# Low parts of the odd layer's q and k weights made by an accumulating DMA instead of a VectorE subtraction

## The chip, the cores and the metric

One core of a Trainium2 chip runs the kernel. The metric is device time in microseconds (us) of one execution; for the kernel before the runs gave 977.92 and 978.41 us, median 978.16. The profile is of one execution, and its times count from that execution's first instruction.

## The reference

A trunk of two layers over 256 tokens of width 2048, all in float32. The even layer joins sparse attention and stick-breaking attention; the odd layer is differential attention with eight heads:

```python
def _odd_layer(x, w_in, ...):
    q, k, v, gate = _split(x @ w_in, ODD_SIZES)          # 4 x 2048 columns
    o = _diff_attn(q, k, v, ...) * jax.nn.silu(gate)     # per head two q and two k of 128, one v of 256
    return _layer_norm(DEEPNORM_ALPHA * x + o @ w_out, ln_g, ln_b)
```

What the change touches is the product of x with the 4096 columns of q and k in the odd layer.

## The kernel before, in words

Products are made on TensorE from numbers in two parts. `split` (L125) turns a float32 tile w into a high part h (a cast to float32r on ScalarE, L126) and a low part l = w - h (a subtraction on VectorE, L127). A product then takes three matmuls: h with the high part of x, h with the low part of x, l with the high part of x.

The weights come once from HBM, in tiles of 128 x 2048 float32 (1 MB). `load_split` (L146) takes a raw tile (three buffers, `wr`), loads it by a DMA from SyncE's queue (L150), and for each half of 1024 columns takes a buffer `wh` and a buffer `wl` (four of each, so four halves or two tiles in all) and splits into them.

In the odd layer's q and k stage, `diff_proj` (L745) calls `ws_pair` (L185) for q and for k of a head, each of two `ws_block`s (L176). A block is one weight tile with 16 chunks of 128 x 128; each chunk is the stationary operand of three matmuls over the 256 tokens (L181 to L183), 48 matmuls to a block. So a head has four blocks, eight halves, and there are eight heads: 32 tiles, 64 halves. L182 is the last reader of a `wh` buffer, L183 of a `wl` buffer. After each block, stages of the attention of the heads before (`diff_attn`, L758) are let in: scores, softmax (`softmax_rows`, L333), transposes, the product with v.

The q and k tiles are then turned by `rope` on VectorE (L297 to L300) and split again. Before this stage lies the odd layer's v projection (`odv` in the names), behind it the gate projection (`odg`) and the output projection (`oo`); these go through `xs_group` with `load_split`, as do the even layer's projections.

Each engine works its own queue in order, and so does SyncE's DMA queue; a framework places instructions on the queues and inserts the waits. The trace shows the loads, casts and subtractions of a tile well ahead of the matmuls that use it, as far as buffers are free. GpSimd (POOL) does only four memsets' worth of setup at the start.

Of the kernel before, what the change touches and what calls it, by code (L numbers as in the profile page):

```python
# [11 lines left out]
F32R = mybir.dt.float32r  # L12
# [4 lines left out]
SEQ = 256  # L17
# [14 lines left out]

# columns of ev_w_in: q kc vc ks vs kw vw gates gate_a qb kb vb gate_b
_SIZES = (1024, 256, 256, 256, 256, 256, 256, 24, 1024, 1024, 1024, 1024, 1024)
_NAMES = ("qa", "kc", "vc", "ks", "vs", "kw", "vw", "ga", "gate_a", "qb", "kb", "vb", "gate_b")
_OFF = dict(zip(_NAMES, np.cumsum((0,) + _SIZES[:-1]).tolist()))
# stationary-weight column blocks of the even layer, in the order they are used
EV_WS = (["kc", "vc", "ks", "kw"], "qa", "qb", "kb", "gate_a", "gate_b")
EV_XS_W = 390

# packed constants: name -> (offset, width)
_CW = (("cosq", 256), ("sinq", 256), ("cosk", 256), ("sink", 256), ("mpos", 256), ("mneg", 256),
# [41 lines left out]
def hybrid_trunk(ctx: ExitStack, tc: tile.TileContext, a):  # L84
# [9 lines left out]
    NU = 28  # L94
    # the one table set with all of Exp, Ln, Abs, Square, Copy and Identity
    nc.scalar.preload_act_table_set("natural_log_exp_and_others")
# [19 lines left out]

    # ---- zeros through the tensor engine while the first loads are under way, so that its clock is up
    zero = cpool.tile([P, 512], mybir.dt.bfloat16, name="zero")
# [4 lines left out]

    # ---- splitting float32 into two parts of 12 bits each, exactly
    def split(h, l, src):  # L125
# [3 lines left out]
    def mm3(o, lhs, rhs, start, stop):  # L129
        """o += lhs.T @ rhs, both in parts"""  # L130
        (ah, al), (bh, bl) = lhs, rhs
        nc.tensor.matmul(o, ah, bh, start=start, stop=False, skip_group_check=True)
        nc.tensor.matmul(o, ah, bl, start=False, stop=False, skip_group_check=True)
        nc.tensor.matmul(o, al, bh, start=False, stop=stop, skip_group_check=True)

    # ---- weights: one DMA per tile, then the two parts
    def raw_tile(n):
# [5 lines left out]
    def unit_part(name, n):  # L143
        return unit(name, [1024], F32R)[:, :n]

    def load_split(src, n, alloc=part, pieces=None, m=1):  # L146
        """pieces(j): called before each part of a half, which is then loaded and split by itself"""
        raw = raw_tile(n)
# [14 lines left out]

    # work in stages, one stage of each after every block of a projection
    staged = []
# [9 lines left out]

    def ws_block(src, ps, xh, xl):  # L176
        """ps[cols, tokens] = W[:, 128 cols].T @ x.T"""
        parts = load_split(src.rearrange("p k c -> p (k c)"), 2048)
        for k in range(NK):
            h, l = (t.rearrange("p (k c) -> p k c", c=P)[:, k % 8, :] for t in parts[k // 8])  # L180
            nc.tensor.matmul(ps, h, xh(k), start=(k == 0), stop=False)  # L181
            nc.tensor.matmul(ps, h, xl(k), start=False, stop=False)  # L182
            nc.tensor.matmul(ps, l, xh(k), start=False, stop=(k == NK - 1))  # L183

    def ws_pair(src, i, name, xh, xl):  # L185
        ps = acc(name)
        for c in range(2):
            ws_block(src[i + c], ps[:, c * SEQ:(c + 1) * SEQ], xh, xl)
            tick()
        return ps.rearrange("p (c t) -> p c t", c=2)  # L190
# [4 lines left out]
    def xs_mm(o, t, parts, half, k0, w, xh, xl, start, stop, c0=0):  # L195
        """o[tokens of t, cols] += x[:, two k] @ W[two k, cols]"""
        h, l = (p.rearrange("p (k c) -> p k c", c=w) for p in parts[half])
# [8 lines left out]
    def xs_group(src, w, name, xh, xl, ahead=None):  # L206
        """ps[t][tokens, cols] = x @ W[:, w cols]"""
        ps = [acc(f"{name}{t}") for t in range(NT)]
# [11 lines left out]
    def xs_apart(src, name, xh, xl, in_units, orders, ready, n_last=1, m=1):  # L220
        """like xs_group, one token tile after the other, the weights kept; ready(t, c0, ps) after each"""
        parts = [None] * 4
# [12 lines left out]

    # ---- constants
    cst = cpool.tile([P, NCST], F32, name="cst")
# [5 lines left out]

    # ---- x transposed, in parts
    def new_lhs(name):
# [30 lines left out]
    def load_constants():  # L276
        nc.sync.dma_start(cst, a["cst"])
        nc.sync.dma_start(sml, a["sml"])
        # lambda = exp(lq1.lk1) - exp(lq2.lk2) + lambda_init, negated, on every partition
        lqk = wk("lqk", [4, HD])  # L280
# [9 lines left out]

    # ---- helpers
    def rope(ps, cos, sin, out):
        """ps, out: [128 d, 2, 256 tokens]"""
        t1 = wk("rope1", [2, SEQ])
# [7 lines left out]
    def log_sigmoid_parts(g, w, tag):  # L302
        """e = ln(1 + exp(-|g|))"""
        e = wk(tag, [512])[:, :w]
# [17 lines left out]
    def rsqrt(out, v, n, name):  # L322
        """out = v ** -0.5, one Newton step after exp(-ln(v) / 2)"""
        y = small.tile([P, n], F32, name=name + "y")
# [8 lines left out]
    def softmax_rows(ps, n, mask, name):  # L333
        """ps: [128 q, 2, n] negated scaled scores -> unnormalised p and 1/sum for both."""
        sm = wk(name, [2, 256])
# [10 lines left out]
    def transposed(p, t, ps):  # L346
        """p: [128 q, (t+1)*128 keys] of query tile t into ps[keys, 3*128]: k0 t0 | k0 t1 | k1 t1"""
        for k in range(t + 1):
            o = (t + k) * P
            nc.tensor.transpose(ps[:, o:o + P], p[:, k * P:(k + 1) * P], ident)  # L350

    def add_pv(o, v, pT, start, stop):
        """o[d, 256 q] += v.T @ p.T over both key tiles"""
        nc.tensor.matmul(o, v(0), pT[:, 0:256], start=start, stop=False, skip_group_check=True)
        nc.tensor.matmul(o[:, P:], v(1), pT[:, 256:384], start=False, stop=stop, skip_group_check=True)

    # =========================== even layer ===========================
    ws, xs = a["ev_ws"], a["ev_xs"]
    # token-major columns: gates | vs | vw | vb
    vsw = [unit(f"vsw{i}", [NT, 512], F32R) for i in range(2)]  # L360
# [23 lines left out]

    kvT = unit("kvT", [2, 2, SEQ])  # compressed-branch k, v: [d, (k v), head, token]
    for i in range(2):
        ps = ws_pair(ws, 2 * i, f"kc{i}", xh, xl)
        nc.scalar.copy(kvT[:, i], ps)
    kr = [unit(f"kr{i}", [2, 2, SEQ], F32R) for i in range(2)]  # roped keys: [d, head, (select window), token]
    for i in range(2):  # L390
# [4 lines left out]

    # compression MLPs
    kcmpT = cpool.tile([P, 2, NCMP], F32, name="kcmpT")
    # compressed values: their three products of parts in one pass, the parts at rows 0, 32 and 64
    vcmp = cpool.tile([STACK, 2, HD], F32R, name="vcmp")
# [62 lines left out]

    # native sparse attention, two heads at a time
    oT = new_lhs("oT")
    hold = {}

    def held(i):
        """for the attention of heads 2i and 2i+1 of all 16"""
        if i // 2 not in hold:
# [13 lines left out]
    def nsa_attn(i, qc, qs):  # L483
        while 0 not in made:
            yield
        kv = i // 2
        # compressed branch
        sc = ps_s("sc")
# [18 lines left out]

        # selected and window branches
        def scores(h):
# [30 lines left out]
        nc.scalar.copy(pT[64:64 + NCMP], tc_[:NCMP, :])  # L540
        pk0 = [unit(f"pk0{j}", [2, 2, SEQ], F32R) for j in range(2)]  # [key, (select window), head, query]
        pk1 = [wk(f"pk1{j}", [2, 2, P], P, F32R) for j in range(2)]
# [72 lines left out]
    def gate_pair(i):  # L615
        """o = attention * silu(gate), in parts, for heads 2i and 2i+1 of all 16"""
        ps = ws_pair(ws, 32 + 2 * i, f"gate{i}", xh, xl)
# [20 lines left out]
    def cols(halves, c):  # L638
        """columns c * 512 ... of a row of 2048 kept in two units"""
        return halves[c // 2][:, c % 2 * 512:(c % 2 + 1) * 512]  # L640

    # ---- output projection, residual and layer norm
    def load_gb(g_src, b_src):
# [8 lines left out]
    def out_layer(wout, lhs, resid, name, finish, g=None, n_last=1):  # L652
        """resid[t] = alpha * resid[t] + lhs @ wout (times g), then finish(t, its mean and 1 / deviation)"""
        oh, ol = lhs_of(lhs)
# [46 lines left out]
    def normalise(t, scale, bias):  # L701
        """resid[t] becomes the normalised row, its scaled and shifted transpose goes to yT"""
        for c in range(4):
# [17 lines left out]

    # =========================== odd layer ===========================
    yh, yl = lhs_of(yT)
# [21 lines left out]
    def diff_proj(h):  # L745
        ps = ws_pair(ws, 4 * h, f"q{h}", yh, yl)
        q = wk("qr", [2, SEQ])
        rope(ps, C("cosq"), C("sinq"), q)
        ps = ws_pair(ws, 4 * h + 2, f"k{h}", yh, yl)
        k = wk("qc", [2, SEQ])  # L750
# [86 lines left out]
    def store(t, scale, bias):  # L837
        """resid[t] is r * g: r * g * scale + (g * bias + b)"""
        last = t == NT - 1
# [27 lines left out]
def _layout(x, ev_w_in, ev_pe_k, ev_pe_v, ev_w1_k, ev_w2_k, ev_w1_v, ev_w2_v, ev_w_out, ev_ln_g, ev_ln_b,  # L867
# [3 lines left out]
    def grouped(w, width):  # L871
        """[2048, n * width] -> [n, 128, 16, width]"""
        n = w.shape[1] // width
# [53 lines left out]
```

## Time and profile before

| | |
|---|---|
| median of the runs | 978.16 us (977.92 and 978.41) |
| span of the profiled execution, first to last instruction | 976.2 us |
| TensorE (PE) busy | 966.6 us, 99% |
| VectorE (DVE) busy | 668.7 us, 69% |
| ScalarE (ACT) busy | 505.6 us, 52% |
| GpSimd (POOL) busy | 1.2 us |
| moved by the DMA engines | 180.8 MB, 185 GB/s on the mean |
| q and k stage of the odd layer | about 582 to 783 us |

The profile has no total of its own beside the span; the runs' median lies 2.0 us above the span. PE stands for matmuls and PEld for the weight loads that overlap them. A DMA share of 1 means that all 16 DMA engines are busy all the time. In names such as `wl<-wr,wh` the tile written stands in front, the tiles read behind, and L127 is line 127 of the kernel before. Granted clock is given in parts of TensorE's full speed.

### The profile page before, as it was taken

The numbers are of one execution on the slowest core, as the hardware profiler recorded it, in microseconds if no ns is written. First come the engines' busy times: TensorE is split into PE (matmuls) and PEld (weight loads), VectorE is DVE, ScalarE is ACT, GpSimd is POOL, SyncE is SP. The second block draws the span as 40 slices with busy tenths as digits, with TensorE's granted clock in tenths as the row PEclk, the third lists the DMA queues.
The fourth block names the chain that finished last, engine by engine and source line by source line (L and its number), as shares of the span: only waits on it lengthen the run. The fifth ranks groups of instructions, "written<-read, shape, count | busy, mean of one in ns | idle before, by whom it ended". The sixth has DMA issues, their size and how long they took to land.

```text
span 976.2 us, 15916 instructions
## 1 busy us (share of the span) xinstructions
PE 966.6 (99%) x6497; PEld 891.6 (91%) x6497; DVE 668.7 (69%) x1107; ACT 505.6 (52%) x812; POOL 1.2 (0%) x8
## 2 busy tenths in 40 slices
PE   8999999999999999999999999999999999999998
PEld 6999999999999999988888889999999988888886
DVE  6544577695766856666598556777778776667676
ACT  5544444475657856535473443455545556664340
POOL 0000000000000000000000000000000000000000
PEclk9999999999999999999999999999999999999999
DMA  8765546643334345756547555544544445557542
GB/s 306 256 207 195 186 169 249 257 138 121 136 123 141 130 174 177 277 193 229 180 150 266 207 176 178 189 156 170 173 167 154 160 168 177 191 193 258 194 151 87
DMA packets 30457, 180.80 MB, mean 185 GB/s; under 512 B 3504, under 2 KB 5296, under 8 KB 11952
## 3 DMA queue, kind: packets, MB, share of 16 engines
q1 hardware_dynamic: 30384, 179.79, 52.3%
q8 instruction: 51, 0.84, 0.3%
q14 instruction: 22, 0.18, 0.1%
HBM read 177.68 MB, written 2.10 MB: 184 GB/s over the span
## 4 chain that ended last, share of the span: by engine, by line
PE 96%; DMA 1%; DVE 1%; ACT 1%; SPq 0%; issue 0%; DVEq 0%; ACTq 0%
PE k L182 3%; PE k L183 3%; PE k L181 3%; PE gate L183 3%; PE q L182 3%; PE gate L182 3%; PE gate L181 3%; PE q L181 3%; PE q L183 3%; PE oo L204 3%; PE oo L202 3%; PE oo L203 3%; PE odv L203 3%; PE odg L202 3%; PE odv L202 3%; PE odg L203 3%
## 5 line engine op out<-in xcount | busy, mean ns | idle before, releaser
L127 DVE TENSOR_TENSOR wl<-wr,wh 128x1024 fp32r<-128x1024 f32 (+3 forms) x330 | 383.2, 1166 | 225.1 <-ACT wh L126 217.9
L126 ACT CAST wh<-wr 128x1024 fp32r<-128x1024 f32 (+3 forms) x330 | 329.7, 1003 | 349.6 <-PE eo L204 40.9
L181 PE MATMUL q<-yTh,wh 128*128 128x256 f32 x256 | 72.9, 285 | 0.0
L181 PE MATMUL gate<-xTh,wh 128*128 128x256 f32 x256 | 72.8, 284 | 0.0
L183 PE MATMUL gate<-xTh,wl 128*128 128x256 f32 x256 | 72.5, 283 | 0.0
L181 PE MATMUL k<-yTh,wh 128*128 128x256 f32 x256 | 72.4, 283 | 0.0
L182 PE MATMUL k<-yTl,wh 128*128 128x256 f32 x256 | 72.4, 283 | 0.0
L183 PE MATMUL k<-yTh,wl 128*128 128x256 f32 x256 | 72.4, 283 | 0.0
L182 PE MATMUL gate<-xTl,wh 128*128 128x256 f32 x256 | 72.4, 283 | 0.0
L183 PE MATMUL q<-yTh,wl 128*128 128x256 f32 x256 | 72.4, 283 | 0.0
L182 PE MATMUL q<-yTl,wh 128*128 128x256 f32 x256 | 72.4, 283 | 0.0
L204 PE MATMUL oo<-wh,oT1l 128*128 128x512 f32 (+1 forms) x144 | 52.7, 366 | 0.0
L203 PE MATMUL oo<-wl,oT1h 128*128 128x512 f32 (+1 forms) x144 | 52.7, 366 | 0.0
L202 PE MATMUL oo<-wh,oT1h 128*128 128x512 f32 (+1 forms) x144 | 52.7, 366 | 0.0
L202 PE MATMUL odg<-wh,yTh 128*128 128x512 f32 x128 | 50.3, 393 | 0.0
L202 PE MATMUL odv<-wh,yTh 128*128 128x512 f32 x128 | 50.1, 392 | 0.0
L202 PE MATMUL eo<-wh,oTh 128*128 128x512 f32 x128 | 50.0, 391 | 0.0
L203 PE MATMUL odv<-wl,yTh 128*128 128x512 f32 x128 | 50.0, 390 | 0.0
L204 PE MATMUL odv<-wh,yTl 128*128 128x512 f32 x128 | 49.9, 390 | 0.0
L203 PE MATMUL eo<-wl,oTh 128*128 128x512 f32 x128 | 49.9, 390 | 0.0
L204 PE MATMUL odg<-wh,yTl 128*128 128x512 f32 x128 | 49.9, 390 | 0.0
L203 PE MATMUL odg<-wl,yTh 128*128 128x512 f32 x128 | 49.8, 389 | 0.0
(287 smaller groups left out, 2494.0 us busy)
## 6 DMA issues: line engine op xcount, KB each, us to landing
wr<-in_ev_ws_dram SPq DMA_DIRECT2D x48, 1024.0 KB, 4.8
wr<-in_od_xs_dram SPq DMA_DIRECT2D x32, 1024.0 KB, 4.8
wr<-in_od_ws_dram SPq DMA_DIRECT2D x32, 1024.0 KB, 4.9
wr<-in_ev_wo_dram SPq DMA_DIRECT2D x16, 1024.0 KB, 4.8
wr<-in_od_wo_dram SPq DMA_DIRECT2D x16, 1024.0 KB, 4.9
wr<-in_ev_xs_dram SPq DMA_DIRECT2D x12, 780.0 KB, 4.6
w<-in_w_dram SPq DMA_DIRECT2D x8, 512.0 KB, 8.4
wr<-in_ev_xs_dram SPq DMA_DIRECT2D x6, 390.0 KB, 6.7
```

Of the source, the lines that this page charges most:

```text
L126: nc.scalar.copy(h, src)
L127: nc.vector.tensor_sub(l, src, h.bitcast(F32))
L181: nc.tensor.matmul(ps, h, xh(k), start=(k == 0), stop=False)
L182: nc.tensor.matmul(ps, h, xl(k), start=False, stop=False)
L183: nc.tensor.matmul(ps, l, xh(k), start=False, stop=(k == NK - 1))
L202: nc.tensor.matmul(o, xh(k)[:, s], h[:, j, cs], start=(start and j == 0), stop=False)
L203: nc.tensor.matmul(o, xh(k)[:, s], l[:, j, cs], start=False, stop=False)
L204: nc.tensor.matmul(o, xl(k)[:, s], h[:, j, cs], start=False, stop=(stop and j == 1))
```

## The change: what it does, and the diff

In the odd layer's q and k stage alone, a tile is prepared by a new function `load_added`. ScalarE writes the negative of the high part into the `wl` buffer (the scaled copy rounds to float32r as the cast does), then the high part into `wh` as before. An accumulating DMA, issued from GpSimd's queue, then adds the raw half to the `wl` buffer in place, which leaves w - h there. VectorE's subtraction is gone for these 64 halves; all other weights are split as before. The buffers and their numbers are the same. The diff also drops comments, which are left out here.

```diff
+    def load_added(src, n):
+        raw = raw_tile(n)
+        nc.sync.dma_start(raw, src)
+        out = []
+        for s in range(2):
+            d = slice(s * (n // 2), (s + 1) * (n // 2))
+            h, m = part("wh", n // 2), part("wl", n // 2)
+            nc.scalar.activation(m, raw[:, d], AF.Copy, scale=-1.0)
+            nc.scalar.copy(h, raw[:, d])
+            nc.gpsimd.dma_start(m, raw[:, d], accum_op=ALU.add)
+            out.append((h, m))
+        return out
...
-    def ws_block(src, ps, xh, xl):
+    def ws_block(src, ps, xh, xl, load=None):
-        parts = load_split(src.rearrange("p k c -> p (k c)"), 2048)
+        parts = (load or load_split)(src.rearrange("p k c -> p (k c)"), 2048)
...
-    def ws_pair(src, i, name, xh, xl):
+    def ws_pair(src, i, name, xh, xl, load=None):
-            ws_block(src[i + c], ps[:, c * SEQ:(c + 1) * SEQ], xh, xl)
+            ws_block(src[i + c], ps[:, c * SEQ:(c + 1) * SEQ], xh, xl, load)
...
     def diff_proj(h):
-        ps = ws_pair(ws, 4 * h, f"q{h}", yh, yl)
+        ps = ws_pair(ws, 4 * h, f"q{h}", yh, yl, load_added)
...
-        ps = ws_pair(ws, 4 * h + 2, f"k{h}", yh, yl)
+        ps = ws_pair(ws, 4 * h + 2, f"k{h}", yh, yl, load_added)
```

## Rows read from the trace of the kernel before

**Rows 1.** The page: span, busy time and share of each engine, instructions.

```profile
span 976.2 us, 15916 instructions
PE 966.6 (99%) x6497; PEld 891.6 (91%) x6497; DVE 668.7 (69%) x1107; ACT 505.6 (52%) x812; POOL 1.2 (0%) x8
```

**Rows 2.** The page: shares of the span in the chain that ended last.

```profile
PE 96%; DMA 1%; DVE 1%; ACT 1%; SPq 0%; issue 0%; DVEq 0%; ACTq 0%
```

**Rows 3.** Busy time by stretch (start:end length), clock, DMA share, GB/s; then one head.

```profile
568.00:760.00 192.00, 192.00 (x1551) 189.59 (x1550) 139.57 (x249) 94.01 (x172) 0.00 (x0) 1.00 0.49 171
633.00:658.60 25.60, 25.60 (x217) 25.60 (x216) 19.95 (x40) 13.22 (x28) 0.00 (x0) 1.00 0.46 163
```

**Rows 4.** Instructions by tile, q and k: duration ns min/median/max, first and last start.

```profile
L181 PE MATMUL q<-yTh,wh x256: 277/283/365, 582.0 to 769.8; 128*128 128x256 f32 x128
...
L183 PE MATMUL k<-yTh,wl x256: 282/283/286, 593.8 to 782.8; 128*128 128x256 f32 x128
```

**Rows 5.** Timeline of ScalarE, 575 to 591 us: start, duration, idle time before and releaser.

```profile
575.45 1.05 ACT L126 CAST wh<-wr 128x1024 fp32r<-128x1024 f32 x1 [3.02 <-PE odv L204]
576.81 1.06 ACT L126 CAST wh<-wr 128x1024 fp32r<-128x1024 f32 x1 [0.30 <-PE odv L204]
...
580.89 1.05 ACT L126 CAST wh<-wr 128x1024 fp32r<-128x1024 f32 x1 [0.77 <-PE odv L204]
...
582.73 1.05 ACT L126 CAST wh<-wr 128x1024 fp32r<-128x1024 f32 x1
585.00 1.05 ACT L126 CAST wh<-wr 128x1024 fp32r<-128x1024 f32 x1 [1.22 <-PE q L182]
587.88 1.05 ACT L126 CAST wh<-wr 128x1024 fp32r<-128x1024 f32 x1 [1.83 <-PE q L182]
590.76 1.05 ACT L126 CAST wh<-wr 128x1024 fp32r<-128x1024 f32 x1 [1.83 <-PE q L182]
```

**Rows 6.** Groups on VectorE in one head, 633.0 to 658.6: busy, mean ns | idle before.

```profile
L127 DVE TENSOR_TENSOR wl<-wr,wh 128x1024 fp32r<-128x1024 f32 x8 | 9.8, 1225 | 4.3 <-ACT wh L126 4.3
```

**Rows 7.** Groups on ScalarE in the same head.

```profile
L126 ACT CAST wh<-wr 128x1024 fp32r<-128x1024 f32 x9 | 9.4, 1050 | 10.4 <-PE q L182 6.3 <-PE k L182 4.1
...
L771 ACT ACTIVATE sm<-sm,smst 128x256 f32<-128x256 f32 x1 | 0.5, 510 | 0.9 <-DVE smst L770 0.9
...
L126 ACT CAST q<-qr 128x256 fp32r<-128x256 f32 x1 | 0.4, 400 | 0.0
```

**Rows 8.** Timeline of ScalarE: first softmax instruction, and the next cast.

```profile
643.24 0.40 ACT L341 ACTIVATE sm<-sm,smst 128x128 f32<-128x128 f32 x1
...
646.33 1.05 ACT L126 CAST wh<-wr 128x1024 fp32r<-128x1024 f32 x1
```

**Rows 9.** Waits of SyncE's DMA queue in the same head: us in total, times, longest.

```profile
SPq L150 <- DVE wl L127: 17.6, 3, 6.5
SPq L150 <- DVE smst L343: 6.5, 1, 6.5
```

**Rows 10.** DMA issues: count, size of each, median us from issue to landing.

```profile
wr<-in_od_ws_dram SPq DMA_DIRECT2D x32, 1024.0 KB, 4.9
...
out_dram<-x SPq DMA_DIRECT2D x6, 256.0 KB, 2.5
...
lngb<-in_od_b_dram SPq DMA_DIRECT2D x2, 512.0 KB, 9.2
...
out_dram<-x SPq DMA_DIRECT2D x4, 128.0 KB, 2.2
```

**Rows 11.** The stretch with the highest DMA rate shown, as rows 3.

```profile
10.00:20.00 10.00, 8.39 (x46) 7.74 (x45) 8.26 (x11) 8.00 (x12) 0.00 (x0) 1.00 1.03 396
```

## Prediction

> **What bounds the kernel now.** I read the busy times first, then the chain of waits, then the stage that the change touches, then the queues that feed it. The page gives PE 966.6 of 976.2 us busy while VectorE has 668.7 and ScalarE 505.6 [rows 1], and the chain that ended last is 96% PE, 1% VectorE, 1% DMA [rows 2]. So TensorE sets the time, and work taken off VectorE buys time only where TensorE waits for VectorE. The table of stretches shows that it does not wait here: between 568 and 760 us PE is busy for 192.00 of 192.00 us, with VectorE at 139.57 [rows 3]. One head of the odd layer takes 25.6 us, in which VectorE works 19.95, ScalarE 13.22, and the 16 DMA engines are busy for a share of 0.46 [rows 3]. The q and k matmuls run from 582.0 to 782.8 us [rows 4]. Those 201 us are what the change can lengthen; it cannot shorten them, because no idle time of PE lies in them.
>
> How far ahead of PE the splitting runs decides what a slower split costs. In the steady state the casts start 2.88 us apart (587.88, 590.76), each released by a q matmul [rows 5]: PE needs 2.88 us for half a weight tile, and four halves fit into the buffers (bufs=4 for wh and for wl). A half's buffer comes free when PE has finished the half four places earlier, so its parts must be ready 3 x 2.88 = **8.64 us** later.
>
> **What is removed.** 64 subtractions (32 tiles, two halves each) of 1.225 us, eight to a head [rows 6]: 78.4 us of VectorE, all beside a busy PE, so worth 0 us.
>
> **What is added on ScalarE.** 64 negations of 128x1024. The profile has no such form. The cast of the same shape takes 1.050 us and is one bound; the scaled copy of 128x256 takes 0.510 against 0.400 for a cast of that size, so 1.050 + 0.110 = 1.16 is the other [rows 7]. I take 1.1, between them: 8 x 1.1 = 8.8 us a head, ScalarE goes from 13.2 to 22.0 of 25.6 us. It does not become the bound, but it has little room: the longest run of softmax work between two casts lasts from 643.24 to 646.33 us [rows 8], 3.1 us in which no negation starts. The negation is queued ahead of the cast on ScalarE, so the cast comes 1.1 us later; 8.64 us of lead cover that.
>
> **What is moved.** wl's last writer is now a DMA. POOL issues 64 of them, one per 3.2 us; it does 1.2 us of work in the whole span [rows 1], so nothing is queued behind these. The raw tile (bufs=3) is now freed by the DMA and not by VectorE. The loads' queue already waits for that release for 17.6 + 6.5 of 25.6 us [rows 9]; what stands behind those waits is the next weight load alone.
>
> **What is added on the DMA engines: the term that decides.** Each accumulating DMA must read 0.524 MB of weights, read 0.524 MB of the tile that it adds to, and write 0.524 MB. No row shows such a transfer. The nearest for transfers out of SBUF are the stores: 128 KB more take 2.5 - 2.2 = 0.3 us more [rows 10], 437 GB/s or 1.2 us for a half, behind a fixed part of 1.9 us (2.2 - 0.3). For loads the best stretch moved 396 GB/s with the engines full (share 1.03) [rows 11], 2.65 us a tile; the q/k stage itself moves 163 GB/s at a share of 0.46 [rows 3], which is 354 GB/s when full, 2.96 us a tile.
> - Lower bound: the second read costs nothing, 1.2 us a half.
> - Taken: the engines read both operands one after the other, 2 x 1.2 = 2.4 us a half, since the diff makes it two reads for one write and the slope comes from the transfer nearest in kind.
> - Upper bound that I can build from a rate: both reads at the stage's load rate, 2.96 us.
> - Farther off stands the slowest half-megabyte in the table, 9.2 us from issue to landing [rows 10]: 64 x 9.2 = 589 us if the adds went one by one, a total of about 1363.
>
> The Trainium skill, "Collectives: The Full Stack", section "The bandwidth ceiling: the fold count and why AG ≠ RS ≠ AR", speaks for two reads: an add inside the DMA engine reads two sources through one read side, at about half a copy's rate. No run here shows it so far. By its 31 GB/s per engine the two reads would take about 2.1 us a half (an estimate from that page), and the sum below would end 19 us earlier, at about 990.
>
> **The sum.** Per head: 8 x 2.4 + 4 x 2.65 = 29.8 us of all 16 engines in 25.6 us. The DMA engines become the bound of this stage. The cast at 585.00 us is the first that a q matmul releases, so the four full ones before it, from 575.45 on, belong to the first two q tiles [rows 5]; the first add can start at about 576.6. From there 64 adds take 153.6 us, and about 30 loads 79.5 (three of the 32 are there already, about one of the next stage comes in between): 576.6 + 233.1 = 809.7, plus 1.9 to land and 2.9 for PE's last half is 814.5. Before, the last k matmul ended at 783.1 (782.8 + 0.28) [rows 4]. So **+31 us**, and the later stages, which use the old split, give nothing back, since PE is full there too. The profiled span of 976.2 becomes 1007.6; the median of the runs lies 2.0 us above that span, so the forecast is **1010 us**. With loads at the stores' 437 GB/s (2.4 us) it is 1002, with 2.96 us it is 1019: 1002 to 1019 is this case's own range. With adds and loads both at 2.96 the stage ends at 860, +77: 1055.
>
> **Rivals.**
> - *The add is hidden (not slower).* If the engine fetches the second operand beside the first, an add costs 1.2 us: 76.8 + 79.5 = 156 us of DMA work in 206. The chain behind a freed buffer is 1.1 for the negation, 1.9 + 1.2 to land, 4.3 us together; even after 3.1 us of softmax work that is 7.4, below 8.64. The time is then 978 to 984, likeliest 980. For it: a share of only 0.46 now. Against it: two operands must come out of SBUF. It decides as long as a half costs less than about 1.9 us, where 64 adds and the loads fill the 206 us. The Trainium skill, "DMA: Bandwidth & Descriptors", section "Anatomy of one DMA — SWDGE (gpsimd) path", has a fixed 2.0 us and the delivered bytes at 436 GB/s for a transfer that POOL issues, an estimate of 3.2 us for a half with no charge for a second read: by that page this rival holds. [...]
> - *Throughput fits, the lead does not.* An add of 2.4 us that also waits for a load of 3.0 lands after 1.9 + 2.4 + 3.0 = 7.3; with the negation and the softmax work it is 11.5 us against 8.64, once a head. 8 x 2.9 = 23 us at most: up to 1001, more likely about 990. Against it: with that queueing the engines are nearly full, which is the forecast again.
> - *The adder itself is the limit.* If the engines add more slowly than they can read twice, PE follows them wholly: at 4.8 us a half 307 + 80 = 387 us, the end moves by 185, some 1163. For it: nothing in this trace tests arithmetic in a DMA. Against it: nothing either, so it holds a real chance.
> - *VectorE's relief helps.* Only waits of PE for wl could be won, and there are none in the stage [rows 3]; under 2% in any case.
>
> **Chances.** A measurement of this kernel tells about 2% from no change, here 19.6 us. Forecast case 0.43 (slower by over 2% 0.34, within 0.09); hidden 0.27 (within 0.26, faster 0.01); lead 0.07 (within 0.06, slower 0.01); slow adder 0.22 (slower); something that helps 0.01 (faster). Together: slower 0.57, within 2% 0.41, faster 0.02. The range runs from 976, which takes in the hidden case, to 1055, the upper bound from a rate. Left out are most of the slow adder and a little below: 0.2.
>
> **What would show it.** In the profile after: a POOL queue with 64 transfers of 512 KB; a DMA share near 1 between 577 and 810 us, and idle time of PE in the q and k matmuls that ends with that queue; time to landing of the adds and of the weight loads well above 4.9 us [rows 10], because they share the engines. VectorE at about 10 us a head, ScalarE at about 22. The forecast is wrong if PE stays busy throughout the stage and the share of DMA stays below 0.8 (then the second read is free), or if PE waits while the landing time of a single add is far above 5 us with a low share (then the adder or its issue is slow). The step that I trust least is the 2.4 us.

## The result: slower by 5.6%, and the profile after

The changed kernel takes 1033.19 us (1031.29 and 1035.10), the one before 978.16: a ratio of 1.0561, 95% interval 1.0539 to 1.0584, or +55 us. That is slower by over 2%, as forecast, and inside the range of 976 to 1055, but 23 us above the 1010 of the forecast.

The page after, first the span and busy times of [rows 1], then TensorE's granted clock, the share of the DMA engines and their GB/s in 40 slices of the span, the DMA queues (packets, MB, share of 16 engines over the span), and the chain that ended last:

```profile
span 1029.5 us, 16087 instructions
PE 980.6 (95%) x6497; PEld 899.1 (87%) x6497; DVE 594.2 (58%) x1043; ACT 565.0 (55%) x876; POOL 56.4 (5%) x72
PEclk9999999999999999999999999999999999999999
DMA  8765467433333457565465899999999974557542
GB/s 299 254 212 192 181 209 263 169 123 124 129 144 138 164 187 264 202 216 191 153 259 187 214 263 266 261 267 263 255 260 272 257 254 165 187 187 252 198 164 82
...
q1 hardware_dynamic: 30384, 179.79, 49.0%
q0 software_dynamic: 9216, 33.56, 17.0%
...
PE 74%; DMA 18%; ACT 4%; issue 2%; DVE 1%; SPq 1%; POOL 0%; DVEq 0%; ACTq 0%; POOLq 0%
DMA wl<-wr 14%; PE gate L198 3%; PE gate L197 3%; PE gate L196 3%; PE oo L219 3%; PE oo L217 3%; PE oo L218 3%; PE odg L217 3%; PE eo L217 3%; PE odg L218 3%; PE odg L219 3%; PE eo L219 3%; PE eo L218 3%; PE odv L218 3%; PE odv L217 3%; PE odv L219 3%
```

The reader is to see three things. VectorE lost 74.5 us of work and nothing was won by it. A new queue, q0, moves 33.56 MB, and it takes 17.0% of 16 engines over the span: 0.170 x 1029.5 / 64 = 2.73 us of all engines for one add of half a megabyte. And the DMA row stands at 9 from slice 24 to slice 32, where the chain, which was 96% PE [rows 2], now runs through `DMA wl<-wr`.

The same places by stretch. The columns, here and below as in [rows 3], are start:end and length, then the busy time of PE, PEld, DVE, ACT and POOL with the number of instructions, then the granted clock, the DMA share and GB/s. The first line is the q/k stage and answers to [rows 3], the second is the time ahead of it, the third the time behind it; the last two lines are the same times in the kernel before:

```profile
577.00:837.00 260.00, 220.62 (x1707) 213.31 (x1706) 80.87 (x219) 161.79 (x259) 54.69 (x64) 0.97 1.02 259
...
0.00:577.00 577.00, 572.40 (x3904) 530.89 (x3905) 380.36 (x624) 308.63 (x480) 1.67 (x9) 1.00 0.55 194
837.00:1029.00 192.00, 187.56 (x890) 154.86 (x888) 132.94 (x200) 94.53 (x139) 0.00 (x0) 1.00 0.52 182
...
0.00:577.00 577.00, 572.32 (x3903) 530.95 (x3904) 381.10 (x625) 307.93 (x480) 1.17 (x8) 1.00 0.55 194
784.00:976.00 192.00, 187.31 (x889) 154.65 (x887) 132.75 (x200) 94.23 (x139) 0.00 (x0) 1.00 0.50 176
```

All of the loss lies in the stage: ahead of it and behind it PE's busy time is the same within 0.3 us. In the stage PE was busy for all of it before; now it is busy for 220.62 of 260.00 us at a DMA share of 1.02. PE's waits there, by line (us in total, times, longest), name the new queue, and the last line has the k matmuls on the low parts, as [rows 4] has them before:

```profile
PE k L198 <- DMA wl<-wr: 19.7, 14, 2.3
PE q L198 <- DMA wl<-wr: 19.4, 14, 3.0
...
L198 PE MATMUL k<-yTh,wl x256: 277/283/416, 598.3 to 836.0; 128*128 128x256 f32 x128
```

39.1 us of PE's idle time end when an add lands; the last k matmul starts at 836.0 us instead of 782.8 [rows 4], 53.2 us later, and the spans differ by 53.3. The other 14 us are busy time: PE's grew by 14.0 us with the same 6497 matmuls, part of it at a lower clock and part at the breaks in their row (last section). Issues and landing, beside [rows 10]:

```profile
wr<-in_od_ws_dram SPq DMA_DIRECT2D x32, 1024.0 KB, 8.8
wl<-wr POOLq DMA_DIRECT2D x64, 512.0 KB, 9.0
```

A weight load of this stage lands after 8.8 us where it took 4.9, an add after 9.0: each queue waits for the other on the same engines.

### The profile page after: what moved, and what is told of

The parts are those of the page before. It is cut to its first block, busy times and chain, and to the rows that moved or that the text cites. A ratio compares the mean times of both kernels' runs of the same rounds, so it can differ in the third digit from the quotient of the medians.

```text
span 1029.5 us, 16087 instructions
## 1 busy us (share of the span) xinstructions
PE 980.6 (95%) x6497; PEld 899.1 (87%) x6497; DVE 594.2 (58%) x1043; ACT 565.0 (55%) x876; POOL 56.4 (5%) x72
## 3 DMA queue, kind: packets, MB, share of 16 engines
q0 software_dynamic: 9216, 33.56, 17.0%
## 4 chain that ended last, share of the span: by engine, by line
PE 74%; DMA 18%; ACT 4%; issue 2%; DVE 1%; SPq 1%; POOL 0%; DVEq 0%; ACTq 0%; POOLq 0%
DMA wl<-wr 14%; PE gate L198 3%; PE gate L197 3%; PE gate L196 3%; PE oo L219 3%; PE oo L217 3%; PE oo L218 3%; PE odg L217 3%; PE eo L217 3%; PE odg L218 3%; PE odg L219 3%; PE eo L219 3%; PE eo L218 3%; PE odv L218 3%; PE odv L217 3%; PE odv L219 3%
## 5 line engine op out<-in xcount | busy, mean ns | idle before, releaser
L126 ACT CAST wh<-wr 128x1024 fp32r<-128x1024 f32 (+3 forms) x266 | 262.7, 992 | 276.8 <-PE eo L219 40.9
L127 DVE TENSOR_TENSOR wl<-wr,wh 128x1024 fp32r<-128x1024 f32 (+3 forms) x266 | 304.8, 1152 | 186.5 <-ACT wh L126 180.0
L156 ACT CAST wh<-wr 128x1024 fp32r<-128x1024 f32 x64 | 66.8, 1044 | 88.2 <-DMA wr<-in_od_ws_dram 61.1
L157 POOL DMA_DIRECT2D wl<-wr x64 | 55.2, 862 | 768.2 <-ACT wl L155 759.0
L198 PE MATMUL q<-yTh,wl 128*128 128x256 f32 x256 | 76.0, 297 | 19.4 <-DMA wl<-wr 19.4
L198 PEld LDWEIGHTS q<-yTh,wl 128*128 128x128 f32 x256 | 50.9, 199 | 22.4 <-DMA wl<-wr 22.3
L198 PEld LDWEIGHTS k<-yTh,wl 128*128 128x128 f32 x256 | 49.8, 194 | 23.4 <-DMA wl<-wr 23.4
L155 ACT ACTIVATE wl<-wr 128x1024 fp32r<-128x1024 f32 x64 | 67.4, 1054 | 3.3 <-PE odv L218 3.3
L197 PEld LDWEIGHTS q<-yTl,wh 128*128 128x128 f32 x256 | 51.0, 199 | 0.0
L196 PEld LDWEIGHTS q<-yTh,wh 128*128 128x128 f32 x256 | 51.0, 199 | 0.0
```

The lines of the kernel that those rows point to most:

```text
L126: nc.scalar.copy(h, src)
L127: nc.vector.tensor_sub(l, src, h.bitcast(F32))
L155: nc.scalar.activation(m, raw[:, d], AF.Copy, scale=-1.0)
L156: nc.scalar.copy(h, raw[:, d])
L157: nc.gpsimd.dma_start(m, raw[:, d], accum_op=ALU.add)
```

## The experiments

The theory was that the 16 DMA engines are full, since an add reads twice. The rivals were the length of the chain (negation, issue, landing against 8.64 us of lead), ScalarE's added work, the arithmetic of the adder, and the conversion of type.

**The transfer without the add.** Leaves out the addition: the transfer overwrites the negated high part with the raw half.

```diff
-            nc.gpsimd.dma_start(m, raw[:, d], accum_op=ALU.add)
+            nc.gpsimd.dma_start(m, raw[:, d])
```

> The 64 transfers stay, issued in the same place, but they copy the raw half over wl instead of adding it: the negation has no effect on the result and the low part is wrong by that. One read and one write of 0.524 MB each. Theory (the 16 DMA engines are full, because an add reads twice): the queue's cost per transfer falls from 2.73 us of all engines (66.4% of 263 us over 64) to about half, 1.3 to 1.4 us; 64 x 1.4 + 94 us of loads = 184 us fits into the stage's 206 us, so the time is 978 to 988 us and the DMA share in the stage about 0.85. Rival (latency: negation, issue by GpSimd, landing, the order on ScalarE): the chain is the same apart from the bytes read, so most of the 55 us stay, 1010 us or more.

Measured: 992.17 us, ratio 1.0152 (1.0131 to 1.0174), 4 us above what the theory allowed, far below the rival's 1010. The queue's line (packets, MB, share over a span of 990.0 us):

```profile
q0 software_dynamic: 9216, 33.56, 9.7%
```

A copy costs 0.097 x 990.0 / 64 = 1.50 us, an add 2.73, 1.8 times as much. With the transfers at that price 40 of the 55 us are gone; the 14 that stay were not expected. In 9.2 of them PE waits for a copy; the copies landed after 3.3 to 10.2 us, 5.2 on the median, and the five waits of over 1.4 us end with copies that took 8.2 to 10.2.

**ScalarE's extra work alone.**

```diff
-            nc.gpsimd.dma_start(m, raw[:, d], accum_op=ALU.add)
+            nc.vector.tensor_add(m, raw[:, d], m.bitcast(F32))
```

> The negation on ScalarE stays, VectorE adds the raw half to wl in place of the DMA. ScalarE has the same 67 us more than before as in the changed kernel. Theory (DMA engines): 976 to 982 us, PE without idle time in the q/k stage. Rival (ScalarE's extra negations and their order on its queue cost the time): at least 1000 us.

Measured: 978.30 us, ratio 1.0005 (0.9995 to 1.0014). The stage, busy times as above:

```profile
577.00:780.00 203.00, 203.00 (x1674) 201.95 (x1674) 152.27 (x282) 162.36 (x258) 0.00 (x0) 1.00 0.48 166
```

ScalarE works 162.36 of 203 us and PE does not wait once. The negations are free; the whole loss comes with the DMA.

**Fewer adds, in rows of four.**

```diff
-        ps = ws_pair(ws, 4 * h + 2, f"k{h}", yh, yl, load_added)
+        ps = ws_pair(ws, 4 * h + 2, f"k{h}", yh, yl)
```

> Only the q tiles are prepared by the accumulating DMA, the k tiles by VectorE's subtraction: 32 adds. Theory (DMA engines full): 32 x 2.73 + 94 = 181 us of DMA work in 206 us, it fits; 978 to 986 us, with a little for two neighbouring q tiles whose adds crowd. Rival (each add brings its own delay): about half of the 55 us, 1005 us.

Measured: 999.15 us, ratio 1.0221 (1.0192 to 1.0249). Neither number: 13 us above the theory's, 6 below the rival's. PE waits for an add in q only, 13.5 us in the stage, none in k. The trace says for which: the first three adds of each row land after 4.5 to 6.0 us, the fourth, which goes out within 1.5 us of a weight load, after 8.4 to 10.0, and each of PE's waits ends with such a fourth add. One of them (queues of GpSimd and SyncE, then PE; start, duration, idle time before and its releaser), and the landing times of all 32, least, median and most:

```profile
611.77 0.33 SPq L165 DMA_DIRECT2D wr<-in_od_ws_dram  x1
611.89 0.86 POOL L157 DMA_DIRECT2D wl<-wr  x1 [2.02 <-ACT q L126]
...
621.93 0.58 PE L198 MATMUL q<-yTh,wl 128*128 128x256 f32 x1 [3.38 <-DMA wl<-wr]
...
DMA to landing us min/median/max: 4.5/5.4/10.0
```

So it is not the number of adds in the stage that counts here, but what an add meets.

**Half of the loads.** Leaves out the second half of each weight tile.

```diff
-        nc.sync.dma_start(raw, src)
+        nc.sync.dma_start(raw[:, :n // 2], src[:, :n // 2])
...
-            d = slice(s * (n // 2), (s + 1) * (n // 2))
+            d = slice(0, n // 2)
```

> Only the first half of each q and k weight tile is loaded (0.5 MB in place of 1 MB), and both halves are made from it: the result is wrong by that, the adds are all there. Theory (adds and loads share the engines, the costs add up): 64 x 2.73 + 47 = 222 us of DMA work in 206 us; about 15 us of the 53 us stay, 990 to 1002 us. Rival (the adds alone are the bound by their rate or their latency, the loads only run beside them): 1020 us or more.

Measured: 999.82 us, ratio 1.0225 (1.0205 to 1.0244), as the theory had it. All 64 adds are there, at 2.79 us each, and 33 of 55 us are gone with 16.8 MB of loads. The stage at a DMA share of 1.03:

```profile
577.00:780.00 203.00, 190.27 (x1520) 185.60 (x1519) 69.32 (x189) 145.73 (x228) 50.72 (x59) 0.99 1.03 226
```

**Bytes or elements.** Two kernels add half the bytes: the first 512 columns as float32, and 1024 elements as bfloat16. The first leaves out half of each addition. The second puts another in its place: it takes 2 KB of each row of `wl` and of `wh` as bfloat16 numbers.

```diff
-            nc.gpsimd.dma_start(m, raw[:, d], accum_op=ALU.add)
+            nc.gpsimd.dma_start(m[:, :n // 4], raw[:, d][:, :n // 4], accum_op=ALU.add)
```

> Each of the 64 adds covers only the first 512 of the 1024 columns (2 KB of each row); the other half of each low part stays the negated high part, and the result is wrong by that. Theory (bytes read): 1.4 us of all engines per add, as much as the plain copy's 1.5; 980 to 994 us. Rival (a fixed cost of each accumulating transfer, its descriptors or its issue): clearly more than 1.4 us per add, 1005 us or more.

```diff
-            nc.gpsimd.dma_start(m, raw[:, d], accum_op=ALU.add)
+            nc.gpsimd.dma_start(m.bitcast(mybir.dt.bfloat16)[:, :n // 2], h.bitcast(mybir.dt.bfloat16)[:, :n // 2], accum_op=ALU.add)
```

> Each of the 64 adds runs over 1024 elements of 2 bytes (the first 2 KB of each row of wl and wh, taken as bfloat16), so it has the bytes of the half-row add and the number of elements of the changed kernel's; the result is wrong by that. The source is wh, so the add waits for the cast too, 1.05 us later. Theory (bytes read): the same cost per add as the half-row run, about 1.4 us, and about its time, 980 to 996 us. Rival (the adder works element by element): 2.7 us per add, 1025 us or more.

Measured: 994.40 us, ratio 1.0169 (1.0144 to 1.0194), and 1003.16 us, ratio 1.0250 (1.0218 to 1.0283). The queue's line of the one, then of the other (spans 996.1 and 1001.1 us):

```profile
q0 software_dynamic: 9216, 16.78, 9.6%
```

```profile
q0 software_dynamic: 9216, 16.78, 9.3%
```

1.49 and 1.46 us an add: with the same bytes the price is the same, though the second adds twice as many elements. So the price does not go by elements. The time of the first is 0.4 us above its range, that of the second 7 us; the second's add waits for the cast as well, and PE's waits there name the negation and the softmax too. The half add reads 2 x 0.262 MB, the copy 0.524 MB, and both cost 1.5 us; the full add reads 1.049 MB and costs 2.73. In these four the price follows the bytes read. An adder that takes bytes at about half the rate of a copy would give the same prices; no run parts that from the second read.

**The conversion of type.**

```diff
-            nc.gpsimd.dma_start(m, raw[:, d], accum_op=ALU.add)
+            nc.gpsimd.dma_start(m.bitcast(F32), raw[:, d], accum_op=ALU.add)
```

> The add's destination is taken as float32 and not as float32r, so source and destination have one type; all else is the changed kernel. Theory (bytes read): no change, 2.7 us per add and 1028 to 1036 us. Rival (a conversion of type on the way is what makes the transfer slow): near 1.2 to 1.5 us per add, below 1000 us.

Measured: 1033.67 us, ratio 1.0571 (1.0547 to 1.0594), 2.72 us an add. The conversion costs nothing.

**Fewer adds, spread out.**

```diff
-            nc.scalar.activation(m, raw[:, d], AF.Copy, scale=-1.0)
+            if s == 0:
+                nc.scalar.activation(m, raw[:, d], AF.Copy, scale=-1.0)
...
-            nc.gpsimd.dma_start(m, raw[:, d], accum_op=ALU.add)
+            if s == 0:
+                nc.gpsimd.dma_start(m, raw[:, d], accum_op=ALU.add)
+            else:
+                nc.vector.tensor_sub(m, raw[:, d], h.bitcast(F32))
```

> The first half of every q and k tile is made by the accumulating DMA, the second by VectorE's subtraction: 32 adds as in the run with q alone, but one in every 5.8 us of PE's work instead of four in a row. Theory (the DMA engines fill up wherever adds crowd, and four buffered halves cannot average over a head): in each 6.4 us one add of 2.8 and one load of 2.8, 5.6 us of DMA work, it fits everywhere; 977 to 984 us. Rival (each add brings a delay of its own, wherever it stands): about 999 us again, as with q alone.

Measured: 993.27 us, ratio 1.0164 (1.0104 to 1.0223): the theory of full engines fails here, 9 us above its number, and adds that crowd each other are not the reason, as they stand apart. The stage shows a DMA share of 0.85 and PE idle for 13.6 us:

```profile
577.00:780.00 203.00, 189.40 (x1525) 187.04 (x1524) 106.22 (x220) 118.82 (x200) 25.00 (x29) 0.98 0.85 229
```

Two of the waits, followed back on ScalarE, GpSimd, SyncE's DMA queue and PE (timelines of one kernel, start, duration, idle time before and its releaser):

```profile
601.29 1.05 ACT L156 ACTIVATE wl<-wr 128x1024 fp32r<-128x1024 f32 x1
602.09 0.33 SPq L150 DMA_DIRECT2D wr<-in_od_ws_dram  x1
602.64 0.86 POOL L159 DMA_DIRECT2D wl<-wr  x1 [4.90 <-ACT wl L156]
...
610.96 0.39 PE L202 MATMUL q<-yTh,wl 128*128 128x256 f32 x1 [1.71 <-DMA wl<-wr]
...
649.54 1.05 ACT L157 CAST wh<-wr 128x1024 fp32r<-128x1024 f32 x1 [0.58 <-PE q L201]
650.49 0.40 ACT L360 ACTIVATE sm<-sm,smst 128x128 f32<-128x128 f32 x1
...
653.58 1.05 ACT L157 CAST wh<-wr 128x1024 fp32r<-128x1024 f32 x1
654.53 1.05 ACT L156 ACTIVATE wl<-wr 128x1024 fp32r<-128x1024 f32 x1
...
655.88 0.86 POOL L159 DMA_DIRECT2D wl<-wr  x1 [5.76 <-DMA wl<-wr]
656.27 0.33 SPq L150 DMA_DIRECT2D wr<-in_od_ws_dram  x1
...
664.82 0.39 PE L202 MATMUL q<-yTh,wl 128*128 128x256 f32 x1 [1.96 <-DMA wl<-wr]
```

The add of 602.64 goes out 0.55 us after a weight load and lands 8.3 us later; PE waits 1.71 us. The add of 655.88 has a load 0.39 us behind it and lands after 8.9 us; its negation (654.53) stands behind softmax work that began at 650.49 as well, and PE waits 1.96 us. PE waits for an add 8 times like that, once a head, and the landing times of all adds are, least, median and most:

```profile
PE q L202 <- DMA wl<-wr: 12.3, 7, 2.8
PE k L202 <- DMA wl<-wr: 1.3, 1, 1.3
...
DMA to landing us min/median/max: 4.5/5.8/9.0
```

All eight waits end with adds that went out within 0.6 us of a weight load and landed after 8.3 to 9.0 us. The other 24 landed after 4.5 to 7.1 us, and PE waited for none. Softmax work stands right ahead of the negation in four of the eight only. With the cast and the negation before it, 1.05 us each, such an add takes over 10 us and does not fit into 8.64. That is the rival of the short lead, with the load beside the add as the main reason. The next run gave it more lead.

**One more buffer.** Both times the same edit, on the kernel of the last run and on the changed kernel, and on the kernel before as a control:

```diff
-        return wpool.tile([P, 1024], F32R, tag=name, bufs=4, name=name)[:, :n]
+        return wpool.tile([P, 1024], F32R, tag=name, bufs=5 if name == "wl" else 4, name=name)[:, :n]
...
-    NU = 28
+    NU = 27
```

> The run with one half of each tile, and one more wl buffer (five in place of four; the pool of 4 KB tiles gives one up, 27 in place of 28). The DMA engines were busy for 0.85 there, not full, and PE waited about 2 us once a head. Theory (the lead: negation behind softmax work on ScalarE, then an add that lands 6 to 9 us later, against 8.64 us): with 2.88 us more of lead that wait goes away, 978 to 986 us. Rival (DMA engines too busy at some point of each head, whatever the lead): it stays, 990 to 996 us.

> The changed kernel with the same fifth wl buffer. Theory (DMA engines full for the whole stage): one half more is ready at the stage's start and no more, 1026 to 1036 us, DMA share still 1. Rival (the lead is what is short here too): 2.88 us more of lead at each of the many waits, 1012 us or less.

> Control: the kernel before with the fifth wl buffer and 27 small tiles. Both theories: no change, 976 to 981 us; anything else is the price of the smaller pool and is taken off the other two.

Measured: 979.46 us, ratio 1.0013 (1.0003 to 1.0023); 1032.09 us, ratio 1.0534 (1.0509 to 1.0558); 978.66 us, ratio 1.0003 (0.9993 to 1.0012). The stage of the first, then of the second:

```profile
577.00:780.00 203.00, 202.55 (x1670) 201.38 (x1669) 117.14 (x250) 131.64 (x225) 26.65 (x31) 1.00 0.97 252
```

```profile
577.00:837.00 260.00, 221.87 (x1687) 213.96 (x1686) 80.21 (x219) 158.74 (x257) 54.34 (x63) 0.96 1.02 260
```

This separates the two causes. With 32 adds the lead was short: 2.88 us more of it takes PE's idle time from 13.6 to 0.45 us, though the engines are busier than in the run without it and an add still takes up to 10.0 us to land. With 64 adds the same buffer gains nothing that can be told: the DMA share is 1.02 with it and without it. No version was faster than the kernel before, whose stage has no idle time of PE to win.

## Why the prediction was right, point by point

- *The subtraction is worth nothing.* Right, and shown: VectorE fell from 668.7 to 594.2 us and the time did not; and with half of the subtractions gone and PE idle for 0.45 us in the stage (one half, five buffers) the time is that of before within 0.23%.
- *The negation costs 1.1 us on ScalarE and is covered.* Right: 1.054 us each in the changed kernel, and free in the run with VectorE's sum. What it does to the lead shows only where an add follows it.
- *Two reads for one write, so the DMA engines become the bound.* Right in mechanism: share 1.02, PE's waits ended by the adds, and no gain from a longer lead. The copy, the half add and the bfloat16 add together tie the price to the bytes; that it is the second read that costs, and not an adder with a rate in bytes, is argued and not shown. The half rate that the Trainium skill gives for adds inside the DMA engine ("Collectives: The Full Stack", section "The bandwidth ceiling: the fold count and why AG ≠ RS ≠ AR") is borne out: 2.73 against 1.50 us, a factor of 1.82. The estimate of 2.1 us from its rate was lower than the 2.73 us measured, and the measurement decides.
- *The size, 2.4 us an add.* This is the term that was off, with the loads. The slope of two stores of 128 and 256 KB was not the rate of transfers beside others: an add takes 2.73 us, 64 x 0.33 = 21 us more than in the sum. The loads were 30 x 2.65 = 79.5 us in the sum; the table of queues for 577 to 840 us gives q1 a share of 35.6% of 263 us, 93.6 us for 34.88 MB, about 33 tiles at 2.81 us:

```profile
q0 software_dynamic: 9216, 33.56, 66.4%
q1 hardware_dynamic: 4787, 34.88, 35.6%
```

  From the first add (576.5 us, forecast 576.6) to the landing of the last (833.3 us), 64 adds and 31 loads at these prices make 175 + 87 = 262 us. They took 257 us, at a share of 1.03; forecast were 233. So the stage grew by 53 us where 31 stood in the sum.
- *One more tile's load of the next stage beside the adds.* Too few by one: two loads for the gate projection were issued before the last add landed, five by 840 us.
- *The hidden case and its decision point, 1.9 us a half.* The copy is the test: 1.50 us, and still 14 us slower. A cost below the point was not enough at four buffers. The point was computed from totals and left out that the two rivals can join: PE's long waits there end with copies that landed late, the mark of a short lead, but no run gave the copy a fifth buffer, so this cause is not shown. The fit of the Trainium skill ("DMA: Bandwidth & Descriptors", section "Anatomy of one DMA — SWDGE (gpsimd) path"), an estimate of 3.2 us for a half, comes near the fastest copy alone, which landed after 3.3 us; the median copy took 5.2, and the fastest add of the changed kernel 5.1. That section gives the fit per DMA and does not say of which kind.
- *The lead.* Given 0.07, it is not what made the changed kernel slow, but it is real: an add that meets a load, once a head, explains the run with one half. That the 15 us there lie between the likely 12 and the 23 at most is partly luck. Those were worked out for 64 adds that land after 7.3 us behind softmax work; the waits came from 32 adds, by landings of 8.3 to 9.0 us, half of them without softmax work.
- *The slow adder.* Not at its 4.8 us a half, as 2.73 were measured, and a price by elements is excluded by the bfloat16 run.

What stays open: whether a longer lead would free the run with q alone and the copy as it freed the run with one half, since neither was made with a fifth buffer; whether the second read or the adder's rate in bytes sets the price; and what the 14 us of PE's busy time would cost if the DMA were not the bound.

## What to carry to other kernels

Before moving arithmetic into a DMA, add up the bytes that the engines read in that stage, both operands of an add, beside the loads that are there already: a share of 0.46 was not room for an add that reads twice its size. Then compare the chain from a freed buffer to the landed result with the lead that the buffers give, at the landing time beside a load that goes out with it, here 8.3 to 10 us, and not at the shortest, here 4.5. Work taken off an engine that nothing waits for was worth nothing here.

## What the runs showed of the hardware that was not expected

- An add issued by GpSimd occupies its queue for 0.86 us, a plain copy of the same shape for 0.53 us (32.9 us for 62). An add of half the bytes takes 0.86 us of the queue too (55.3 us for 64).
- The granted clock fell in four places of the changed kernel's stage, each right behind a wait of PE. In the first (the last column but two is the granted clock) PE was busy for 2.03 of 5 us, and in the next 5 us the clock was 0.66 on the mean, so part of them at 1.2 GHz and not at 2.4:

```profile
590.00:595.00 5.00, 2.03 (x17) 1.82 (x16) 0.00 (x0) 2.00 (x2) 1.72 (x2) 1.00 1.04 214
595.00:600.00 5.00, 5.00 (x32) 5.00 (x31) 1.85 (x3) 2.01 (x2) 0.00 (x0) 0.66 1.05 279
...
605.00:610.00 5.00, 2.72 (x23) 2.51 (x22) 0.00 (x0) 3.95 (x5) 1.73 (x3) 1.00 1.05 235
610.00:615.00 5.00, 5.00 (x44) 5.00 (x44) 2.51 (x4) 2.30 (x3) 1.19 (x2) 1.00 1.05 270
```

  In the other pair of lines, after 2.72 us of work in 5, it stayed at 1.00. An estimate of what makes up the 14 us: a mean clock of 0.993 over 1029.5 us against 0.999 over 976.2 is about 6 us; and at each of the 28 waits the matmul before it has no next one to overlap with (24 of them take 2.88 us, so they start 0.12 us apart, and one lasts 0.28), which is 0.16 us each, together 4.5. The rest was not traced. As the DMA engines set the pace, the runs do not show what either would cost by itself.
